# Multi-query attention on one core: quads of heads, values scaled on VectorE, a staged start and a re-planned order

## The chip, the cores and the metric

One core of a Trainium2 chip. The time is device microseconds of one execution; a kernel's time is the median over its runs. Lower is better. All engines named below are those of the one core: PE (TensorE, matrix products), ACT (ScalarE, exponentials), DVE (VectorE), POOL (GpSimd) and SP (SyncE, which here only issues transfers).

## The reference

Eight batches, sequence 1024, 16 query heads of 64 dimensions, and one key head and one value head that all query heads share. In fp32:

```python
scores = np.matmul(q, k.transpose(0, 1, 3, 2)) / np.sqrt(head_dim)     # q: 8x16x1024x64
weights = np.exp(scores - np.max(scores, axis=-1, keepdims=True))
weights = weights / np.sum(weights, axis=-1, keepdims=True)
attn_out = np.matmul(weights, v)
```

The order of the keys within a batch doesn't matter to the result, as long as values stand in the same order.

## The kernel before

The 16 heads of a batch are taken as 8 pairs; over 8 batches that is 64 pairs (`NP`). A pair's keys are cut in 8 tiles of 128, so there are 512 key tiles, numbered through. A tile's scores for a pair (128 keys by 2 heads by 1024 queries) come in two query halves `c` of 512 queries each, 1024 halves in all.

**One half.** `score` (L382) makes two products, one per head, into one of three score slots in PSUM (`sc0` to `sc2`). An exponential then turns the slot into fp16 weights `wt`: on ScalarE by one ACTIVATE (`exp_act`, L397), or on VectorE (`exp_dve`, L402): `z` for each half (L410), and after the second half four more steps for the whole tile (L421 to L428). A tile on VectorE gives three terms (`wt`, `z`, `m`), which are multiplied with three copies of the values that are scaled by the constants `TERMS`.

**Values.** `value` (L431) multiplies weights with values for a group of 6, 4 or 6 of the 16 blocks of 128 queries (`BLOCKS`), and adds up in one of two accumulators in PSUM. Row 65 of the values is a constant, so the sum of the weights comes with it. A ScalarE tile costs one such product per block, a VectorE tile three. When a group is complete, `reciprocal` (L451) and `normalise` (L456) on VectorE write `osb`, and after the third group SP stores the pair. In the last pair each group is stored by itself.

**The order.** PE, ScalarE and VectorE run in an order that is written out by hand: `plan` (L51) walks through the work with its own costs and due times for each instruction (the constants of L22 to L37), decides which tiles VectorE takes (`vtiles`), and emits scores, exponentials, steps, value products and normalisations sorted by due time. `LAG`, `END` and `END_LAG` say how far value work stays behind the scores, `BACKLOG` and `BACK_END` how much work may stand before VectorE, `LAST` how many last tiles VectorE may not take, `MARGIN` and `WAIT` when PE changes between scores and values. The last 8 tiles (`NKT`) are taken by halves: first all first halves, then all second halves (L105 to L112). On the chip each engine runs its list in order and waits where it must.

**Loads.** They are not in the hand-written order; a scheduler places them on SP and POOL. `begin(w)` (L484) runs when the first score of pair `w` is emitted: it loads pair `w+3` (`load_q`, L331, on POOL, with conversion to fp16), transposes pair `w+2` by DMA (`trans_q`, L341, on SP), and in pairs 2, 4 and 5 of a batch brings the next batch's keys (`load_k`, L299, twice into both halves of the rows, so that each head of a pair has its copy), values (`load_v`, L308) and scaled values (`scale_v`, L313, three instructions on POOL). Keys and values are read with key `c*128 + p` on partition `p`, that is in rows of 64 numbers (256 bytes).

**The start.** `load_first` (L349) brings the first keys and the first pair's queries in fp32 by SP and ACT; beside them pairs 1 and 2 and the first values are loaded. `turn_first` (L360) converts both on VectorE (L364, L367), transposes them on PE into the two accumulator banks (L375, L378), and copies them out on VectorE (keys, L376) and ScalarE (queries, L380).

Of the kernel before, what the change touches and what calls it, by code (L numbers as in the profile page):

```python
# [9 lines left out]
FP32 = mybir.dt.float32  # L10
# [13 lines left out]
MARGIN, WAIT = 0.2, 0.2  # L24
END, END_LAG = 5.0, 0.0
# [5 lines left out]
BACKLOG, BACK_END = 5.6, 3.4  # L31
LAST = 14
WBUFS = 25
ZBUFS = 6
LAG = 1.55
# [15 lines left out]
def plan(NP, NKT):  # L51
# [31 lines left out]
    while p < NP or groups:  # L83
        assert min(pe, dve) < 2e3
        if pe <= dve:
# [161 lines left out]
def kernel(  # L247
# [21 lines left out]
    qp = ctx.enter_context(tc.tile_pool(name="qp", bufs=4))  # L269
    qtp = ctx.enter_context(tc.tile_pool(name="qtp", bufs=3))  # L270
# [28 lines left out]
    def load_k(b):  # L299

        st = kst.setdefault(b, {})
        st["k16"] = kvp.tile([P, NKT, 2, D], FP16, tag="k16", name=f"k16{b}")
        for r in range(2):
            nc.gpsimd.dma_start(  # L304
                out=st["k16"][:, :, r, :], in_=k[b].rearrange("(c p) d -> p c d", p=P)
            )

    def load_v(b):  # L308
        st = kst[b]
        st["vn"] = kvp.tile([P, NKT, D], FP32, tag="vn", bufs=1, name=f"vn{b}")  # L310
        nc.sync.dma_start(out=st["vn"], in_=v[b].rearrange("(c p) d -> p c d", p=P))

    def scale_v(b):  # L313
# [3 lines left out]
        for x, c in zip(st["v"], TERMS):  # L317
            if c == 1.0:
                nc.gpsimd.tensor_copy(out=x[:, :, 0:D], in_=st["vn"])  # L319
            else:  # L320
                nc.gpsimd.tensor_scalar(  # L321
                    out=x[:, :, 0:D], in0=st["vn"], scalar1=c, scalar2=None, op0=ALU.mult)
# [7 lines left out]

    def load_q(p):  # L331
        if p >= NP or p in qn:
            return
        b, hp = divmod(p, HP)
        qn[p] = qp.tile([P, NKT, 2 * D], FP16, tag="qn", name=f"qn{p}")
        nc.gpsimd.dma_start(  # L336
            out=qn[p],
            in_=q[b, :, 2 * hp : 2 * hp + 2, :].rearrange("(c p) h d -> p c (h d)", p=P),
        )

    def trans_q(p):  # L341
        if p >= NP:
            return
        qt[p] = qtp.tile([P, NKT + 1, P], FP16, tag="qt", name=f"qt{p}")[:, 0:NKT, :]
        nc.sync.dma_start_transpose(
            out=qt[p], in_=qn[p].rearrange("p c x -> p (c x)")
        )

    def load_first():  # L349
        st = kst.setdefault(0, {})  # L350
        st["kn"] = osbp.tile([P, NKT, D], FP32, tag="osb", name="kn")
        nc.sync.dma_start(out=st["kn"], in_=k[0].rearrange("(c p) d -> p c d", p=P))
        st["qf"] = osbp.tile([P, NKT, 2 * D], FP32, tag="osb", name="qf")
        for c in range(NQC):
# [3 lines left out]
            )  # L358

    def turn_first():  # L360
        st = kst[0]
        k16 = kvp.tile([P, NKT, 2, D], FP16, tag="k16", name="k160")
        for r in range(2):
            nc.vector.tensor_copy(out=k16[:, :, r, :], in_=st["kn"])  # L364
        qn[0] = qp.tile([P, NKT, 2 * D], FP16, tag="qn", name="qn0")
        for c in range(NQC):
            nc.vector.tensor_copy(  # L367
                out=qn[0][:, 4 * c : 4 * c + 4, :], in_=st["qf"][:, 4 * c : 4 * c + 4, :]
            )
# [3 lines left out]
        qt[0] = qtp.tile([P, NKT + 1, P], FP16, tag="qt", name="qt0")[:, 0:NKT, :]  # L373
        for c in range(NKT):
            nc.tensor.transpose(kps[:, c, :], k16[:, c, :, :].rearrange("p r d -> p (r d)"), ident)  # L375
        nc.vector.tensor_copy(out=st["k2t"], in_=kps)  # L376
        for c in range(NKT):
            nc.tensor.transpose(qps[:, c, :], qn[0][:, c, :], ident)  # L378
            if c % 4 == 3:
                nc.scalar.copy(out=qt[0][:, c - 3 : c + 1, :], in_=qps[:, c - 3 : c + 1, :])  # L380
# [103 lines left out]
    def begin(w):  # L484
        load_q(w + 3)
        trans_q(w + 2)
# [63 lines left out]
```

The softmax here doesn't subtract the row's maximum and nothing guards it: scores larger than these inputs give would overflow.

## Time and profile before

| what | value |
|---|---|
| median of 12 runs | 774.1 us (772.11 to 776.3) |
| profiled execution, its own time | 775.15 us |
| its span on the core | 773.4 us |
| PE busy | 734.2 us (95%) |
| DVE busy | 714.4 us (92%) |
| ACT busy | 756.3 us (98%) |
| POOL busy | 108.4 us (14%) |
| exponentials on ScalarE / `z` on VectorE | 820 / 204 |

A line of the timeline gives the start and the length in us, the engine, the line of the code, the operation, output and inputs with shapes, how many instructions are merged, and in brackets how long the engine was idle just before and what released it. A row of the groups gives busy time, the mean ns of one instruction, and the idle time before the group. Instructions of one engine overlap, so a mean duration is longer than the pace at which they follow each other.

### The profile page before, as it was taken

How to read it: one execution, taken by the hardware profiler on the slowest of the kernel's cores; microseconds unless marked ns; L12 is line 12 of the kernel's file. 1: busy time of each engine (PE TensorE's matmuls, PEld its weight loads, DVE VectorE, ACT ScalarE, POOL GpSimd, SP SyncE). 2: the span in 40 equal slices, each digit the busy share in tenths (PEclk: the TensorE clock that was granted, in tenths of full speed). 3: DMA queues.
4: the chain of work that ended last, by engine and by line, in shares of the span. 5: the costliest groups of instructions: out<-in, count | busy, mean ns of one | idle time of the engine just before them, and what ended most of it. 6: DMA issues, size and time to landing. Idle time of an engine off the chain costs nothing.

```text
span 773.4 us, 29898 instructions
## 1 busy us (share of the span) xinstructions
PE 734.2 (95%) x13520; PEld 489.1 (63%) x13520; DVE 714.4 (92%) x1001; ACT 756.3 (98%) x823; POOL 108.4 (14%) x113
## 2 busy tenths in 40 slices
PE   5999999999999999999999999999999999999997
PEld 1466666566666666566666676665666676666675
DVE  5999999999899998998999999999999989999972
ACT  6999999999999999999999999999999999999997
POOL 6500013000130101200013001030001201000000
PEclk9999999999999999999999999999999999999999
DMA  9945586355875457665694545764546465741322
GB/s 153 134 70 98 83 125 115 78 99 97 98 121 106 79 97 121 102 97 71 111 124 84 97 86 83 125 114 67 97 80 115 98 104 78 110 99 43 84 57 83
DMA packets 231137, 75.07 MB, mean 97 GB/s; under 512 B 164449, under 2 KB 231009, under 8 KB 231009
## 3 DMA queue, kind: packets, MB, share of 16 engines
q1 hardware_dynamic: 149600, 54.15, 32.0%
q0 software_dynamic: 80080, 18.36, 26.2%
q8 instruction: 105, 1.72, 0.9%
q10 hardware_dynamic: 1328, 0.66, 0.3%
q14 instruction: 24, 0.19, 0.1%
HBM read 39.58 MB, written 33.55 MB: 95 GB/s over the span
## 4 chain that ended last, share of the span: by engine, by line
ACT 55%; PE 17%; DVE 15%; issue 11%; DMA 1%; ACTq 0%; DVEq 0%
ACT wt L398 55%; PE acc L441 9%; PE sc L386 8%; DVE z L410 6%; DVE m L427 2%; DVE m L428 2%; DVE wt L421 2%; DVE u L424 2%; DVE osb L463 2%; DMA qf<-in_q_dram 1%; DVE rec L454 0%; DVE qn L367 0%; PE qps L378 0%; ACT qt L380 0%; ACTq L355 0%
## 5 line engine op out<-in xcount | busy, mean ns | idle before, releaser
L398 ACT ACTIVATE wt<-sc 128x1024 f16<-128x1024 f32 x820 | 753.9, 1238 | 5.2 <-PE sc L386 4.9
L441 PE MATMUL acc<-vals,wt 128*128 128x65 f16 x8192 | 378.4, 194 | 1.1 <-DVE osb L463 0.8
L441 PEld LDWEIGHTS <-wt 128*128 128x128 f16 x8192 | 296.1, 97 | 125.5 <-issue 124.9
L386 PE MATMUL sc<-qt,k2t 64*128 64x512 f16 x2048 | 349.1, 388 | 27.0 <-ACT wt L398 15.6
L410 DVE TENSOR_SCALAR z<-sc 128x1024 uint16<-128x1024 f32 x204 | 249.0, 1220 | 22.5 <-PE sc L386 20.0
L386 PEld LDWEIGHTS <-k2t 64*128 64x128 f16 x2048 | 107.6, 94 | 107.0 <-issue 61.2
L336 POOL DMA_DIRECT2D qn<-in_q_dram x63 | 58.7, 932 | 550.0 <-DMA qt<-qn 517.7
L427 DVE TENSOR_TENSOR m<-u 128x2048 f16<-128x2048 f16 x102 | 124.6, 1222 | 1.8
L428 DVE TENSOR_TENSOR m<-z,m 128x2048 f16<-128x2048 f16 x102 | 123.1, 1207 | 0.4
L441 PE MATMUL acc<-vals,z 128*128 128x65 f16 x1632 | 100.1, 194 | 0.0
L463 DVE TENSOR_TENSOR osb<-acc,rec 128x384 f32<-128x384 f32 (+1 forms) x192 | 97.2, 506 | 1.3
L441 PE MATMUL acc<-vals,m 128*128 128x65 f16 x1632 | 98.2, 193 | 0.0
L441 PEld LDWEIGHTS <-z 128*128 128x128 f16 x1632 | 69.2, 97 | 19.5 <-issue 19.5
L441 PEld LDWEIGHTS <-m 128*128 128x128 f16 x1632 | 68.3, 97 | 20.7 <-issue 20.7
L424 DVE TENSOR_SCALAR u<-z 128x2048 uint16<-128x2048 uint16 x102 | 73.6, 721 | 0.0
L421 DVE TENSOR_SCALAR wt<-z 128x2048 uint16<-128x2048 uint16 x102 | 71.1, 697 | 2.1 <-ACT wt L398 0.4
L454 DVE RECIPROCAL rec<-acc 128x6 f32<-128x6 f32 (+1 forms) x192 | 35.1, 183 | 21.4 <-PE acc L441 21.3
L321 POOL TENSOR_SCALAR vals<-vn 128x512 f16<-128x512 f32 x16 | 28.3, 1771 | 26.3 <-PE acc L441 23.7
L304 POOL DMA_DIRECT2D k<-in_k_dram x14 | 13.3, 956 | 0.2 <-issue 0.2
L319 POOL CAST vals<-vn 128x512 f16<-128x512 f32 x8 | 7.5, 939 | 3.6 <-DMA vn<-in_v_dram 3.5
L375 PE MATMUL kps<-ident,k 128*128 128x128 f16 x8 | 1.0, 311 | 6.0 <-DVE k L364 6.0
L380 ACT COPY qt<-qps 128x512 f16<-128x512 f16 x2 | 1.2, 586 | 5.0 <-PE qps L378 5.0
(14 smaller groups left out, 8.0 us busy)
## 6 DMA issues: line engine op xcount, KB each, us to landing
out_dram<-osb SPq DMA_DIRECT2D x63, 512.0 KB, 3.5
qn<-in_q_dram POOLq DMA_DIRECT2D x63, 256.0 KB, 4.7
vn<-in_v_dram SPq DMA_DIRECT2D x8, 256.0 KB, 3.2
k<-in_k_dram POOLq DMA_DIRECT2D x14, 128.0 KB, 6.0
qt<-qn SPq DMA_TRANSPOSE x63, 3.8
qf<-in_q_dram ACTq DMA_DIRECT2D x2, 256.0 KB, 5.4
out_dram<-osb SPq DMA_DIRECT2D x2, 192.0 KB, 2.1
kn<-in_k_dram SPq DMA_DIRECT2D x1, 256.0 KB, 4.4
```

The costliest lines, as they stand in the source:

```text
L321: nc.gpsimd.tensor_scalar(out=x[:, :, 0:D], in0=st["vn"], scalar1=c, scalar2=None, op0=ALU.mult)
L336: nc.gpsimd.dma_start(out=qn[p], in_=q[b, :, 2 * hp : 2 * hp + 2, :].rearrange("(c p) h d -> p c (h d)", p=P),)
L386: nc.tensor.matmul(sc[t, c][:, h, :], kst[p // HP]["k2t"][64 * h : 64 * h + 64, j, :], qt[p].rearrange("p c x -> p (c x)")[64 * h : 64 * h ...
L398: nc.scalar.activation(out=wt[t][:, :, c * QC : (c + 1) * QC], in_=sc.pop((t, c)), func=EXP, scale=ascale)
L410: nc.vector.tensor_scalar(out=z[:, :, c * QC : (c + 1) * QC], in0=sc.pop((t, c)), scalar1=vscale, scalar2=(15 + math.log2(C0)) * ONE, op0= ...
L421: lambda: V.tensor_scalar(out=wt[t].bitcast(U16), in0=z, scalar1=0xFC00, scalar2=None, op0=ALU.bitwise_and),
L424: lambda: V.tensor_scalar(out=u, in0=z, scalar1=1023, scalar2=14 << 10, op0=ALU.bitwise_and, op1=ALU.bitwise_or),
L427: lambda: V.tensor_tensor(out=m, in0=h, in1=h, op=ALU.mult),
L428: lambda: V.tensor_tensor(out=m, in0=z.bitcast(FP16), in1=m, op=ALU.mult),
L441: nc.tensor.matmul(acc[p, grp][:, o : o + D + 1], w[:, h, i * P : (i + 1) * P], kst[p // HP]["v"][k][:, j, 0 : D + 1], start=(n == 0 and o ...
L454: nc.vector.reciprocal(out=rec[p, grp][:, 0 : a.shape[1]], in_=a[:, :, D])
L463: nc.vector.tensor_tensor(out=o.rearrange("p i (h d) -> p (i h) d", h=2)[:, BLOCKS[grp] : BLOCKS[grp + 1], :], in0=a[:, :, 0:D], in1=rec.p ...
```

## The change

- **Constants of the planner**: `MARGIN`, `WAIT`, `END`, `END_LAG`, `BACKLOG`, `BACK_END`, `LAG` get other values, and a new `SPLIT` of 4 takes the place of 8 for the number of last tiles that are taken by halves.
- **Quads**: pairs 0 and 1 are still moved singly; from pair 2 on, one load and one DMA transpose bring two pairs (4 heads), at every second pair. The loads run `w+4`, the transposes `w+2` ahead. Buffers: two of double size, for loaded and for transposed queries each (4 and 3 single ones before). The score reads its queries as four pieces of 128.
- **Rows of keys and values**: key `p*8 + c` on partition `p`, so that a partition's 8 keys are one row of 2 KB. The same in values.
- **Scaling of values**: three instructions on VectorE in the hand-written order in place of three on POOL; the first batch's at the start of pair 1.
- **Start**: POOL converts one half of the first keys, VectorE the other. Keys and queries are transposed and copied by halves, keys' copies on ScalarE, queries' on VectorE. The loads of pair 1 and of the first values wait for the first keys and the first query half, because POOL copies one element of these into their buffers; the load of pairs 2 and 3 comes after the transposes.
- **POOL** is now in the hand-written order too.

```diff
-MARGIN, WAIT = 0.2, 0.2
-END, END_LAG = 5.0, 0.0
+MARGIN, WAIT = 0.29, 0.18
+END, END_LAG = 4.84, 0.175
...
-BACKLOG, BACK_END = 5.6, 3.4
-LAST = 14
+BACKLOG, BACK_END = 5.67, 4.09
+LAST, SPLIT = 14, 4
...
-LAG = 1.55
+LAG = 1.37
...
-                if nt < NT - NKT:
+                if nt < NT - SPLIT:
...
-    qp = ctx.enter_context(tc.tile_pool(name="qp", bufs=4))
-    qtp = ctx.enter_context(tc.tile_pool(name="qtp", bufs=3))
+    qp = ctx.enter_context(tc.tile_pool(name="qp", bufs=2))
+    qtp = ctx.enter_context(tc.tile_pool(name="qtp", bufs=2))
...
-                out=st["k16"][:, :, r, :], in_=k[b].rearrange("(c p) d -> p c d", p=P)
+                out=st["k16"][:, :, r, :], in_=k[b].rearrange("(p c) d -> p c d", p=P)
...
         for x, c in zip(st["v"], TERMS):
-            if c == 1.0:
-                nc.gpsimd.tensor_copy(out=x[:, :, 0:D], in_=st["vn"])
-            else:
-                nc.gpsimd.tensor_scalar(
-                    out=x[:, :, 0:D], in0=st["vn"], scalar1=c, scalar2=None, op0=ALU.mult)
+            nc.vector.tensor_scalar(
+                out=x[:, :, 0:D], in0=st["vn"], scalar1=c, scalar2=None, op0=ALU.mult)
...
+    def quad(p):
+
+        return (p,) if p < 2 else (p & ~1, p | 1)
+
+    def queries(pool, tag, p, more):
+
+        t = pool.tile([P, 2 * NKT + more, P], FP16, tag=tag, name=f"{tag}{p}")
+        return t[:, 0 : NKT * len(quad(p)), :]
...
     def trans_q(p):
...
+        ps = quad(p)
+        t = queries(qtp, "qt", p, 1)
         nc.sync.dma_start_transpose(
-            out=qt[p], in_=qn[p].rearrange("p c x -> p (c x)")
-        )
+            out=t, in_=qn[ps[0]].rearrange("p c x -> p (c x)")
+        )
+        for r, x in enumerate(ps):
+            qt[x] = t.rearrange("p (c r) x -> p c r x", r=len(ps))[:, :, r, :]
...
+        nc.gpsimd.tensor_copy(out=st["k16"][:, :, 1, :], in_=kn)
...
+        for x, y in ((qn[1][:, 0, 0:1], kn), (st["vn"][:, 0, 0:1], st["qf"])):
+            nc.gpsimd.tensor_copy(out=x, in_=y[:, 0, 0:1])
...
+        nc.vector.tensor_copy(out=k16[:, :, 0, :], in_=st["kn"])
+        for c in range(NQC):
+            x = slice(4 * c, 4 * c + 4)
+            for i in range(4 * c, 4 * c + 4):
+                nc.tensor.transpose(
+                    kps[:, i, :], k16[:, i, :, :].rearrange("p r d -> p (r d)"), ident)
+            nc.scalar.copy(out=st["k2t"][:, x, :], in_=kps[:, x, :])
+            nc.vector.tensor_copy(out=qn[0][:, x, :], in_=st["qf"][:, x, :])
+            for i in range(4 * c, 4 * c + 4):
+                nc.tensor.transpose(qps[:, i, :], qn[0][:, i, :], ident)
+            nc.vector.tensor_copy(out=qt[0][:, x, :], in_=qps[:, x, :])
...
-                qt[p].rearrange("p c x -> p (c x)")[
-                    64 * h : 64 * h + 64, c * QC : (c + 1) * QC
-                ],
+                qt[p][64 * h : 64 * h + 64, 4 * c : 4 * c + 4, :],
...
     def begin(w):
-        load_q(w + 3)
-        trans_q(w + 2)
+        if w % 2 == 0:
+            if w + 4 < NP:
+                load_q(w + 4)
+            if w + 2 < NP:
+                trans_q(w + 2)
+        if w == 1:
+            scale_v(0)
...
     load_first()
+    load_v(0)
     load_q(1)
-    load_v(0)
-    load_q(2)
-    trans_q(1)
-    scale_v(0)
-    with tc.manual_schedule(engines={ENG.PE, ENG.Activation, ENG.DVE}):
+    with tc.manual_schedule(engines={ENG.PE, ENG.Activation, ENG.DVE, ENG.Pool}):
         turn_first()
+        load_q(2)
+        trans_q(1)
```

More of the change, by code (lines that the diff above doesn't have):

```diff
@@ L309, in load_v @@
         st = kst[b]
-        st["vn"] = kvp.tile([P, NKT, D], FP32, tag="vn", bufs=1, name=f"vn{b}")
-        nc.sync.dma_start(out=st["vn"], in_=v[b].rearrange("(c p) d -> p c d", p=P))
+        if "vn" not in st:
+            st["vn"] = kvp.tile([P, NKT, D], FP32, tag="vn", bufs=1, name=f"vn{b}")
+        nc.sync.dma_start(out=st["vn"], in_=v[b].rearrange("(p c) d -> p c d", p=P))
     def scale_v(b):
@@ L329, in trans_k @@
         )
+    def quad(p):
[3 more added lines that the diff above has]
+        return t[:, 0 : NKT * len(quad(p)), :]
     def load_q(p):
[L332 to L335, printed above, removed]
+        ps = quad(p)
+        b, hp = divmod(ps[0], HP)
+        if p not in qn:
+            qn[p] = queries(qp, "qn", p, 0)
         nc.gpsimd.dma_start(
[L337 to L338 removed]
+            out=qn[ps[0]].rearrange("p (c r) x -> p c (r x)", r=len(ps)),
+            in_=q[b, :, 2 * hp : 2 * hp + 2 * len(ps), :].rearrange(
+                "(c p) h d -> p c (h d)", p=P),
         )
     def trans_q(p):
[L342 to L344 removed]
+        ps = quad(p)
+        t = queries(qtp, "qt", p, 1)
         nc.sync.dma_start_transpose(
[L346 removed]
+            out=t, in_=qn[ps[0]].rearrange("p c x -> p (c x)")
         )
+        for r, x in enumerate(ps):
+            qt[x] = t.rearrange("p (c r) x -> p c r x", r=len(ps))[:, :, r, :]
     def load_first():
         st = kst.setdefault(0, {})
[L351 to L352 removed]
+        kn = osbp.tile([P, NKT, D], FP32, tag="osb", name="kn")
+        nc.sync.dma_start(out=kn, in_=k[0].rearrange("(p c) d -> p c d", p=P))
         st["qf"] = osbp.tile([P, NKT, 2 * D], FP32, tag="osb", name="qf")
@@ L358, in load_first @@
             )
+        st["k16"] = kvp.tile([P, NKT, 2, D], FP16, tag="k16", name="k160")
+        nc.gpsimd.tensor_copy(out=st["k16"][:, :, 1, :], in_=kn)
+        st["kn"] = kn
+        qn[0] = queries(qp, "qn", 0, 0)
+        qn[1] = queries(qp, "qn", 1, 0)
+        st["vn"] = kvp.tile([P, NKT, D], FP32, tag="vn", bufs=1, name="vn0")
+        for x, y in ((qn[1][:, 0, 0:1], kn), (st["vn"][:, 0, 0:1], st["qf"])):
+            nc.gpsimd.tensor_copy(out=x, in_=y[:, 0, 0:1])
+        qt[0] = queries(qtp, "qt", 0, 1)
     def turn_first():
         st = kst[0]
[L362 to L368, printed above, removed]
-            )
+        k16 = st["k16"]
         kps = psp.tile([P, NKT, P], FP16, tag="acc0", name="kps")
@@ L372, in turn_first @@
         st["k2t"] = kvp.tile([P, NKT + 1, P], FP16, tag="k2t", name="k2t0")[:, 0:NKT, :]
[L373 to L380, printed above, removed]
+        nc.vector.tensor_copy(out=k16[:, :, 0, :], in_=st["kn"])
[9 more added lines that the diff above has]
+            nc.vector.tensor_copy(out=qt[0][:, x, :], in_=qps[:, x, :])
     def score(t, c, s):
```

## The prediction

> **What bounds the kernel now.** I read the page from its first part (busy shares), then the ScalarE rows of the timeline, then the idle-time column of the groups, then the start and the end of the timeline.
>
> ```profile
> span 773.4 us, 29898 instructions
> PE 734.2 (95%) x13520; PEld 489.1 (63%) x13520; DVE 714.4 (92%) x1001; ACT 756.3 (98%) x823; POOL 108.4 (14%) x113
> ...
> L398 ACT ACTIVATE wt<-sc 128x1024 f16<-128x1024 f32 x820 | 753.9, 1238 | 5.2 <-PE sc L386 4.9
> ...
> L410 DVE TENSOR_SCALAR z<-sc 128x1024 uint16<-128x1024 f32 x204 | 249.0, 1220 | 22.5 <-PE sc L386 20.0
> ...
> L454 DVE RECIPROCAL rec<-acc 128x6 f32<-128x6 f32 (+1 forms) x192 | 35.1, 183 | 21.4 <-PE acc L441 21.3
> ```
>
> ScalarE (ACT) is busy 98% and waits 5.2 us in all; the two large waits of VectorE (DVE) cost nothing as long as ScalarE is fed. The 1238 ns of one exponential is not its pace, since instructions overlap. The pace comes from the unbroken runs of the ScalarE timeline:
>
> ```profile
> 31.54 130.44 ACT L398 ACTIVATE wt<-sc 128x1024 f16<-128x1024 f32 x142 [0.32 <-PE sc L386]
> 162.15 108.27 ACT L398 ACTIVATE wt<-sc 128x1024 f16<-128x1024 f32 x118 [0.17 <-PE sc L386]
> 271.19 152.79 ACT L398 ACTIVATE wt<-sc 128x1024 f16<-128x1024 f32 x166 [0.77 <-PE sc L386]
> 424.40 3.77 ACT L398 ACTIVATE wt<-sc 128x1024 f16<-128x1024 f32 x4 [0.42 <-PE sc L386]
> 428.32 16.66 ACT L398 ACTIVATE wt<-sc 128x1024 f16<-128x1024 f32 x18
> 446.38 90.86 ACT L398 ACTIVATE wt<-sc 128x1024 f16<-128x1024 f32 x99 [1.40 <-PE sc L386]
> 552.00 216.44 ACT L398 ACTIVATE wt<-sc 128x1024 f16<-128x1024 f32 x236 [0.17 <-PE sc L386]
> ```
>
> The last run has 236 exponentials in 216.44 us; the shortest one takes 1.02, so the other 235 cost (216.44 - 1.02)/235 = 0.9166 us each. The exponentials fill 9.39 (first start) to 768.44 (552.00 + 216.44), 759.05 us. At full pace 820 need 1.02 + 819 x 0.9166 = 751.7, so 7.3 us are stalls. The span is thus start 9.39, exponentials 751.7, stalls 7.3, tail 773.4 - 768.44 = 5.0. I forecast each of the four.
>
> **Exponentials: -5.5 us.** The planner's new constants fix another written order. In the built order VectorE takes 105 of 512 tiles where it took 102, so ScalarE has 814 exponentials: 6 x 0.9166 = 5.5 less.
>
> **Stalls of the old order: -3.5 us.** Counting exponentials along the runs, those after the 164th, 282nd, 448th, 470th and 584th pause. At these places the planner's own due times for ScalarE leave gaps: its order brings the score late there. The new due times have no gap. What they cost is taken from the trace: recorded waits 0.17 + 0.77 + 0.42 + 1.40 + 0.17 = 2.93, and an exponential after a pause doesn't overlap its forerunner, which hides about 0.1 more each: 3.5. The other 3.8 us of stalls (2.0 of them before 34 us, the rest around a clock dip at 540 us and short waits) I leave as they are.
>
> **VectorE: heavier, the price is in the bursts.** It gets
> - 3 more tiles. The five rows of an exponential by VectorE sum to 249.0 + 124.6 + 123.1 + 73.6 + 71.1 = 641.4 us for 102 tiles, 6.29 each; overlap cuts that (all rows sum to 776, busy is 714.4, factor 0.92) to 5.8: +17.4 us.
> - 24 value scalings that GpSimd (POOL) did. No row of VectorE has them; the nearest is the two conversions of the same shape (128x512 f32 to f16) at the start, 0.76 for two, so 0.38 each: +9.1 us, in eight bursts of three, 1.1 us each. Bounds 0.34 and 0.53 each.
> - Relief: written orders that put an instruction right behind the one whose result it needs cost 0.11 (m by m at 407.06 comes 1.25 after the one at 405.81 whose result it reads; with an unrelated neighbour 1.14). Of such pairs the built order has 123 before and 19 after: 104 x 0.11 = -11.4.
> - Relief from GpSimd. In the trace u takes 1.09 beside a value scaling at 409.21 on GpSimd and 0.65 without:
>
> ```profile
> 403.52 0.65 DVE L424 TENSOR_SCALAR u<-z 128x2048 uint16<-128x2048 uint16 x1
> ...
> 409.21 1.61 POOL L321 TENSOR_SCALAR vals<-vn 128x512 f16<-128x512 f32 x1 [7.90 <-PE acc L441]
> ...
> 410.28 1.09 DVE L424 TENSOR_SCALAR u<-z 128x2048 uint16<-128x2048 uint16 x1
> ```
>
> By the row, the excess of mean over median is (721 - 684) x 102 = 3.8 us for u and (697 - 686) x 102 = 1.1 for wt: -4.9. The Trainium skill, "SBUF — State Buffer", section "Who interferes with whom", states that a VectorE instruction in a two-port mode and a GpSimd instruction exclude each other for the whole instruction. Taken at its most, all 28.3 + 7.5 = 35.8 us of GpSimd's scaling block VectorE, and the move would make it lighter by 35.8 - 9.1 = 26.7; by the row it becomes heavier by 9.1 - 4.9 = 4.2. I take the row: most of those 35.8 us lie beside instructions that the trace shows undisturbed.
>
> Sum for VectorE: 17.4 + 9.1 - 11.4 - 4.9 = +10.2 us. Between 32 and 745 us it is busy 681.2 of 713, so 31.8 idle; that window shrinks by 9 (5.5 + 3.5), and the remaining idle is about 12.6 us, under 2%. So VectorE keeps up on average, but has nothing to spare behind a burst. What is queued behind one is the next z on VectorE, which holds one of three score slots in PSUM; PE's next score for that slot waits, and PE is in order, so the scores for ScalarE behind it are late. Bounds: 0 (idle time of VectorE takes every burst) and 8 x 1.1 = 9 (each reaches ScalarE whole). ScalarE has up to two finished scores ahead of it, so I take a quarter, nearer the lower end: +2. If that cover is gone it is 9.
>
> **Start: -1.7 us.** Now the chain is qf, cast, transposes, copy, score:
>
> ```profile
> 5.17 0.76 DVE L364 CAST k<-kn 128x512 f16<-128x512 f32 x2 [5.17 <-DMA kn<-in_k_dram]
> ...
> 7.37 0.72 DVE L367 CAST qn<-qf 128x512 f16<-128x512 f32 x1 [1.10 <-DMA qf<-in_q_dram]
> ...
> 8.79 0.59 ACT L380 COPY qt<-qps 128x512 f16<-128x512 f16 x1 [0.72 <-PE qps L378]
> ...
> 9.39 9.27 ACT L398 ACTIVATE wt<-sc 128x1024 f16<-128x1024 f32 x10
> ```
>
> Keys land at 5.15 and the second query half at 7.34, in company with values and two more query loads. In the changed order those wait (one-element copies on GpSimd that read kn and qf), and the keys come in 2 KB rows instead of 256 B. A value load of the same bytes in 256 B rows lands in 3.0 at best (issue to landing of vn: 3.0/3.2/5.9), so keys at 0.73 + 3.0 = 3.7 and query halves at 4.3 and 4.9. The Trainium skill, "DMA: Bandwidth & Descriptors", section "Anatomy of one DMA", gives 2.0 us plus bytes over 436 GB/s: an estimate of 2.6 for 256 KB, keys at 3.3, exponentials 0.4 earlier than by the row. I take the row. From there: GpSimd cast 0.60 (4.3), four key transposes 0.6 (4.9), ScalarE copies half 0.59 (5.5), PE's next key transposes wait for that copy (their line waits on ACT) and end at 6.1; VectorE meanwhile does k, first query cast, first qt copy and second query cast, about 6.4; the last query transposes 0.6 (7.05), and the scores stand behind them in PE's queue; from there to the first exponential 0.65 as now (8.74 to 9.39): 7.7. Bounds: 6.9 (DMA estimate, no queueing) and 9.4 (no gain).
>
> What is late next: the pair-1 queries issue only when qf is there, at about 5 (now 1.42), plus about 1 to issue, 4.7 to land, 1.3 + 3.8 to be transposed, 15.8; pair 1 starts 10.8 us after the first scores, at about 18. Hidden, with 2 us to spare. The first values land by 10, the first value matmul is at 22 or later. The quads (two pairs per load and transpose) halve GpSimd's and SP's issues. In SP's queue a double transpose stands behind stores; it is released when pair w-1 is scored and needed two pairs (23 us) later, against 2 x 3.8 us: hidden, price 0. The score's moving operand is now four pieces of 128; PE waits 27 us before scores anyway, 0.
>
> **Tail: +1.5 us.** Splitting only four last tiles leaves more value work behind the last score: in the built order 128 matmuls (all of pair 63's) instead of 68.
>
> ```profile
> 765.61 0.60 PE L386 MATMUL sc<-qt,k2t 64*128 64x512 f16 x4
> ...
> 766.15 2.09 PE L441 MATMUL acc<-vals,wt 128*128 128x65 f16 x60
> ...
> 768.49 0.42 PE L441 MATMUL acc<-vals,wt 128*128 128x65 f16 x8 [0.26 <-ACT wt L398]
> ```
>
> PE ends 3.3 after the last score now; 60 matmuls take 2.09, so 128 take 4.5, plus 0.53 of scores: 5.0. ScalarE ends about 2.5 after that score, against 2.8. PE thus ends 2.5 after ScalarE instead of 0.5: +2.0. Behind it only one group is normalised instead of two: -0.5. The store of 3.3 us remains.
>
> **Sum.** -5.5 - 3.5 + 2 - 1.7 + 1.5 = -7.2: span 766.2. The profiled run took 775.15 us for 773.4; the runs' median 774.1 is 0.7 over the span, which I keep: 766.9.
>
> **Rivals.**
> 1. Everything is covered: bursts 0 and the start at its lower bound (6.9, -0.8): 764.1. For it: 21.4 us of VectorE's idle is waiting for acc, which is time left over. Against it: those waits stand in the middle of its queue and need not meet a burst.
> 2. The start doesn't get shorter (keys' arrival isn't what ends last, GpSimd's cast and the single file on PE are): first exponential at 9.4 and bursts at half: 766.9 + 1.7 + 2.5 = 771.1. For it: PE's order puts all sixteen transposes ahead of the first score, and one copy between.
> 3. Slower: VectorE becomes the bound. Place: every z behind a burst, in all batches. If the two reliefs don't come (16.3 us), its need rises by 26.5 against 31.8 - 9 = 22.8 of idle, 3.7 too much; and if half of the old idle cannot be filled, since it is waiting for acc or scores, 16 more: stalls +19.7 in place of +2, so 784.6 at worst, 776.6 with 8 of the 16. It decides from 2 + 7.2 = 9.2 us of new stalls on. Against it: the 1.09 beside GpSimd and the 0.11 of dependence are in the trace.
>
> **How the numbers follow.** Chances: the sum above 0.55 (its own range 764.8 to 769), rival 1 0.16, rival 2 0.14, rival 3 0.15. The range runs from 762.5 (a little under rival 1, whose bounds don't add up lower than that by more than 2) to 772.5 (above rival 2), and leaves rival 3 out. 0.2% is 1.5 us, about what tells two times of this kernel apart; within it 0.03, taken from rival 2's upper end and rival 3's lower one: faster 0.84, same 0.03, slower 0.13.
>
> **What would show it.** First exponential at 7.7 and the landing of kn and qf; 814 exponentials at 0.917, no pause after the 164th, 282nd or 470th; three scalings of 0.38 on VectorE and, just behind, ScalarE pauses of a few tenths; u never above 0.8 beside GpSimd except near its DMA issues; PE ending 2.5 after the last exponential. The forecast is wrong if ScalarE shows waits for scores all along the run (then z is late), or if pair 1 or 2 waits for its qt.

## The result and the profile after

The changed kernel takes 765.39 us (median of 8 runs, 764.61 to 767.2) against 774.66 of the kernel before, run beside it: ratio 0.9881, 95% interval 0.9865 to 0.9896. It is 1.2% faster. The forecast was 766.9, with a range of 762.5 to 772.5.

The page of the changed kernel, the lines that answer to those of before (engines, then groups as busy time, mean ns, idle time before them):

```profile
span 764.1 us, 29940 instructions
PE 739.0 (97%) x13616; PEld 486.6 (64%) x13616; DVE 721.3 (94%) x1043; ACT 750.3 (98%) x817; POOL 47.0 (6%) x61
...
L411 ACT ACTIVATE wt<-sc 128x1024 f16<-128x1024 f32 x814 | 747.8, 1244 | 2.3 <-PE sc L401 2.0
...
L423 DVE TENSOR_SCALAR z<-sc 128x1024 uint16<-128x1024 f32 x210 | 256.4, 1221 | 19.2 <-PE sc L401 14.5
...
L467 DVE RECIPROCAL rec<-acc 128x6 f32<-128x6 f32 (+1 forms) x192 | 35.1, 183 | 13.7 <-PE acc L454 13.7
...
L319 DVE TENSOR_SCALAR vals<-vn 128x512 f16<-128x512 f32 x24 | 8.7, 419 | 0.0
```

ScalarE is still busy 98%, with 6 exponentials fewer; VectorE has become busier (94% after 92%). ScalarE's own timeline, all exponentials:

```profile
8.14 13.86 ACT L411 ACTIVATE wt<-sc 128x1024 f16<-128x1024 f32 x15 [0.67 <-PE sc L401]
22.30 1.02 ACT L411 ACTIVATE wt<-sc 128x1024 f16<-128x1024 f32 x1 [0.31 <-PE sc L401]
23.71 2.92 ACT L411 ACTIVATE wt<-sc 128x1024 f16<-128x1024 f32 x3 [0.39 <-PE sc L401]
26.91 87.55 ACT L411 ACTIVATE wt<-sc 128x1024 f16<-128x1024 f32 x95 [0.27 <-PE sc L401]
114.62 139.79 ACT L411 ACTIVATE wt<-sc 128x1024 f16<-128x1024 f32 x152 [0.16 <-PE sc L401]
254.65 502.95 ACT L411 ACTIVATE wt<-sc 128x1024 f16<-128x1024 f32 x548 [0.24 <-PE sc L401]
```

The breaks of 0.8 and 1.4 us that stood at 271 and 446 us are gone. The exponentials fill 8.14 to 757.60 (254.65 + 502.95), 749.46 us. At the pace of before 814 of them need 1.02 + 813 x 0.9166 = 746.2, which leaves 3.25 of stalls. At the start the keys are there at 4.02, where they came at 5.17; at the end PE has 128 products left behind the last score, and ends (759.98) 2.4 after the last exponential:

```profile
4.02 0.43 DVE L385 CAST k<-kn 128x512 f16<-128x512 f32 x1 [4.02 <-DMA kn<-in_k_dram]
...
755.83 4.15 PE L454 MATMUL acc<-vals,wt 128*128 128x65 f16 x128
```

The four terms of the prediction, in us of the profiled executions:

| term | before | after | difference | forecast |
|---|---|---|---|---|
| start (first exponential) | 9.39 | 8.14 | -1.25 | -1.7 |
| exponentials at full pace | 751.7 | 746.2 | -5.5 | -5.5 |
| stalls of ScalarE | 7.3 | 3.25 | -4.1 | -1.5 (-3.5 and +2) |
| tail after the last exponential | 5.0 | 6.5 | +1.5 | +1.5 |
| span | 773.4 | 764.1 | -9.3 | -7.2 |

The forecast was 2.1 us short: 2.6 too little in the stalls, less 0.45 too much at the start. The experiments ask which part of the change made each term.

"Full pace" needs care: 0.9166 is the mean of a long run without a large break, not ScalarE's own step. Taken singly from the trace, the starts mostly follow each other at 0.904 us (536 of 819 steps before and 424 of 813 after are below 0.907). Longer steps go with late scores: they average 0.93 us or more where the score's products ended less than 0.12 us before the exponential's start, and 0.905 to 0.912 where they ended over 0.2 before. At 0.904 the exponentials take 741.4 and 736.0 us and the stalls are 17.7 and 13.5. The differences in the table hold (-5.4 and -4.2), but some 10 us of mostly such small waits are inside its pace.

### The profile page after: what moved, and what is told of

Read it like the earlier page. It is cut to its first block, busy times and chain, and to the rows that moved or that the text cites. A ratio compares the mean times of both kernels' runs of the same rounds, so it can differ in the third digit from the quotient of the medians.

```text
span 764.1 us, 29940 instructions
## 1 busy us (share of the span) xinstructions
PE 739.0 (97%) x13616; PEld 486.6 (64%) x13616; DVE 721.3 (94%) x1043; ACT 750.3 (98%) x817; POOL 47.0 (6%) x61
## 4 chain that ended last, share of the span: by engine, by line
ACT 43%; PE 35%; DVE 16%; issue 5%; DMA 0%; POOL 0%; DVEq 0%; ACTq 0%
ACT wt L411 43%; PE acc L454 20%; PE sc L401 14%; DVE z L423 6%; DVE m L441 2%; DVE m L440 2%; DVE osb L476 2%; DVE u L437 1%; DVE wt L434 1%; DVE vals L319 1%; DVE rec L467 0%; DMA kn<-in_k_dram 0%; PE qps L394 0%; POOL k L369 0%; PE kps L389 0%
## 5 line engine op out<-in xcount | busy, mean ns | idle before, releaser
L401 PE MATMUL sc<-qt,k2t 64*128 64x512 f16 x2048 | 356.6, 388 | 13.9 <-ACT wt L411 6.5
L423 DVE TENSOR_SCALAR z<-sc 128x1024 uint16<-128x1024 f32 x210 | 256.4, 1221 | 19.2 <-PE sc L401 14.5
L401 PEld LDWEIGHTS <-k2t 64*128 64x128 f16 x2048 | 100.8, 93 | 99.6 <-issue 55.1
L441 DVE TENSOR_TENSOR m<-z,m 128x2048 f16<-128x2048 f16 x105 | 126.5, 1205 | 0.0
L454 PE MATMUL acc<-vals,z 128*128 128x65 f16 x1680 | 103.2, 194 | 0.0
L454 PE MATMUL acc<-vals,m 128*128 128x65 f16 x1680 | 94.4, 194 | 0.0
L437 DVE TENSOR_SCALAR u<-z 128x2048 uint16<-128x2048 uint16 x105 | 71.1, 677 | 0.0
L343 POOL DMA_DIRECT2D qn<-in_q_dram x32 | 30.6, 956 | 614.4 <-DMA qt<-qn 613.0
L319 DVE TENSOR_SCALAR vals<-vn 128x512 f16<-128x512 f32 x24 | 8.7, 419 | 0.0
```

The source lines that it names most:

```text
L319: nc.vector.tensor_scalar(out=x[:, :, 0:D], in0=st["vn"], scalar1=c, scalar2=None, op0=ALU.mult)
L343: nc.gpsimd.dma_start(out=qn[ps[0]].rearrange("p (c r) x -> p c (r x)", r=len(ps)), in_=q[b, :, 2 * hp : 2 * hp + 2 * len(ps), :].rearrang ...
L401: nc.tensor.matmul(sc[t, c][:, h, :], kst[p // HP]["k2t"][64 * h : 64 * h + 64, j, :], qt[p][64 * h : 64 * h + 64, 4 * c : 4 * c + 4, :], ...
L423: nc.vector.tensor_scalar(out=z[:, :, c * QC : (c + 1) * QC], in0=sc.pop((t, c)), scalar1=vscale, scalar2=(15 + math.log2(C0)) * ONE, op0= ...
L437: lambda: V.tensor_scalar(out=u, in0=z, scalar1=1023, scalar2=14 << 10, op0=ALU.bitwise_and, op1=ALU.bitwise_or),
L441: lambda: V.tensor_tensor(out=m, in0=z.bitcast(FP16), in1=m, op=ALU.mult),
```

## Experiments

Three sets of four kernels; each set ran on one chip beside the kernel before. The changed kernel itself came out at 0.9881 and, in the second set, at 0.9905, so ratios are compared within a set, and differences of 0.1% to 0.2% are read from the terms of the profile rather than from the ratio. Only the second set held the changed kernel itself; in the first and the third, its nearest kin (without the waits, and with single pairs) stand for it.

### The order alone

The kernel before with nothing but the planner's new constants and `SPLIT`:

```diff
-MARGIN, WAIT = 0.2, 0.2
-END, END_LAG = 5.0, 0.0
+MARGIN, WAIT = 0.29, 0.18
+END, END_LAG = 4.84, 0.175
...
-BACKLOG, BACK_END = 5.6, 3.4
-LAST = 14
+BACKLOG, BACK_END = 5.67, 4.09
+LAST, SPLIT = 14, 4
...
-LAG = 1.55
+LAG = 1.37
...
-                if nt < NT - NKT:
+                if nt < NT - SPLIT:
```

> Only the planner's constants and SPLIT of the change, on the old loads, old start and GpSimd scaling. My theory (the four terms add up): 814 exponentials -5.5 us, the pauses of the old order -3.5, tail +1.5, start unchanged at 9.4: span about 766, ratio to before 0.990. Rival (the denser order only works if GpSimd's scaling no longer disturbs VectorE): new pauses of ScalarE behind every scaling on GpSimd, span 770 or more, ratio 0.995 or more.

Measured: 765.56 us, ratio 0.9881 (0.9868 to 0.9895), span 763.2. ScalarE's timeline in it:

```profile
9.13 9.27 ACT L398 ACTIVATE wt<-sc 128x1024 f16<-128x1024 f32 x10
18.63 4.70 ACT L398 ACTIVATE wt<-sc 128x1024 f16<-128x1024 f32 x5 [0.23 <-PE sc L386]
23.48 1.02 ACT L398 ACTIVATE wt<-sc 128x1024 f16<-128x1024 f32 x1 [0.16 <-PE sc L386]
24.90 731.79 ACT L398 ACTIVATE wt<-sc 128x1024 f16<-128x1024 f32 x798 [0.39 <-PE sc L386]
```

From 24.90 on, 798 exponentials run without a break: (731.79 - 1.02)/797 = 0.9169 each. Stalls are 756.69 - 9.13 - 746.2 = 1.35 us, all before 30 us, though GpSimd still scales the values. (The start is 0.26 earlier than in the profile of before, with the same instructions: that much the landing of the first loads scatters.) The rival falls: the new order needs no relief from GpSimd. It alone is worth the whole gain of the change: in the same set the changed kernel without its waits has 0.9884, and everything but the order, below, 1.0003. More of the stalls go than the 3.5 that I had credited it with: 7.3 - 1.35 = 6.0.

`plan` is plain Python, and run by itself it tells more. The old constants leave seven gaps between ScalarE's due times, 4.8 us in all: 0.49 after the 164th exponential, 1.01 after the 282nd, 0.21 (344th), 0.57 (448th), 1.86 (470th), 0.15 (482nd) and 0.49 (584th). The new constants leave none. Put back one at a time, `END_LAG` and `BACKLOG` don't alter the order, and `END`, `BACK_END` and `SPLIT` alter only its end; `MARGIN`, `WAIT` and `LAG` each bring gaps back, and with these three alone new there is no gap. No run separates them on the chip.

### Everything but the order

The changed kernel with the old constants and the old split put back (the diff above, reversed, on the new loads, start and scaling).

> The whole change except its order: old constants, last eight tiles split. My theory: start -1.25 us as measured, the pauses of the old order come back, VectorE's scaling bursts find more idle time than in the new order and cost 0 to 1: span 772 to 773, ratio 0.998 to 0.999. Rival (the gain is in the loads and in the scaling): span 769 or less, ratio 0.994.

Measured: 774.6 us, ratio 1.0003 (0.9994 to 1.0012), span 772.8.

```profile
27.80 132.80 ACT L411 ACTIVATE wt<-sc 128x1024 f16<-128x1024 f32 x144 [0.29 <-PE sc L401]
160.78 2.86 ACT L411 ACTIVATE wt<-sc 128x1024 f16<-128x1024 f32 x3 [0.17 <-PE sc L401]
164.26 105.94 ACT L411 ACTIVATE wt<-sc 128x1024 f16<-128x1024 f32 x115 [0.63 <-PE sc L401]
270.97 152.58 ACT L411 ACTIVATE wt<-sc 128x1024 f16<-128x1024 f32 x166 [0.77 <-PE sc L401]
423.78 20.27 ACT L411 ACTIVATE wt<-sc 128x1024 f16<-128x1024 f32 x22 [0.23 <-PE sc L401]
446.10 96.39 ACT L411 ACTIVATE wt<-sc 128x1024 f16<-128x1024 f32 x105 [2.05 <-PE sc L401]
542.79 8.47 ACT L411 ACTIVATE wt<-sc 128x1024 f16<-128x1024 f32 x9 [0.29 <-PE sc L401]
551.43 216.44 ACT L411 ACTIVATE wt<-sc 128x1024 f16<-128x1024 f32 x236 [0.17 <-PE sc L401]
```

The first lines of this timeline, not shown, hold 15 + 4 + 1 = 20 exponentials. Counted on, breaks stand after the 164th, 282nd, 448th, 470th and 584th, the very places of the kernel before, with other loads, other buffers and another start. They belong to the order. Two more, after the 167th and the 575th, follow scalings on VectorE (from 158.1 and 536.8 us). The first exponential is at 8.01, but stalls are 8.15: the earlier start (-1.4) is given back partly in stalls (+0.8), and no difference in time is left to see. The span lies in my 772 to 773; the ratio reached neither the rival's 0.994 nor my 0.998. Loads, start and scaling together are worth nothing that can be seen.

### Scaling on GpSimd again

```diff
-            nc.vector.tensor_scalar(
-                out=x[:, :, 0:D], in0=st["vn"], scalar1=c, scalar2=None, op0=ALU.mult)
+            if c == 1.0:
+                nc.gpsimd.tensor_copy(out=x[:, :, 0:D], in_=st["vn"])
+            else:
+                nc.gpsimd.tensor_scalar(
+                    out=x[:, :, 0:D], in0=st["vn"], scalar1=c, scalar2=None, op0=ALU.mult)
```

> The changed kernel with the scaling of values back on GpSimd. My theory (VectorE gets 4 us lighter in sum, the bursts of 1.1 us fall away but each scaling slows one or two VectorE instructions by 0.4): ScalarE's stalls of 3.3 us change by -1.5 to +1, ratio to before 0.987 to 0.990. Rival (exclusion of the two engines for whole instructions): VectorE is blocked for most of GpSimd's 36 us, with 18 us of idle left in the middle of the run: stalls +5 us or more, ratio 0.994 or more.

Measured: 764.04 us, ratio 0.9862 (0.9848 to 0.9875), the lowest of its set and a little under what I expected. Stalls are 2.0 in place of 3.25. Its groups:

```profile
L437 DVE TENSOR_SCALAR wt<-z 128x2048 uint16<-128x2048 uint16 x105 | 75.8, 722 | 0.2
...
L322 POOL TENSOR_SCALAR vals<-vn 128x512 f16<-128x512 f32 x16 | 29.6, 1850 | 1.4
```

`wt` takes 722 ns on average, against 684 in the changed kernel: 105 x 0.038 = 4 us of disturbance by GpSimd, about what the row of before gave, and far from the 36 us of GpSimd's work. Between 32 and 735 us VectorE is idle 703 - 683.8 = 19.2 us, against 17.7 with the scaling on VectorE. That VectorE pays for the whole length of GpSimd's work is refuted; whether one of the two stands still while the other works is not decided by these rows. Moving the scaling to VectorE was no gain. By the profile it was a small loss, 1.25 us of stalls, and the breaks behind the bursts are gone; but two profiles of the changed kernel differ by 1.4, and the ratio overlaps that of the kernel without the waits (0.9884) in the same set.

### The start: without the waits

The changed kernel without the two one-element copies:

```diff
-        for x, y in ((qn[1][:, 0, 0:1], kn), (st["vn"][:, 0, 0:1], st["qf"])):
-            nc.gpsimd.tensor_copy(out=x, in_=y[:, 0, 0:1])
```

> The changed kernel without the two one-element copies, so that the loads of pair 1 and of the first values start at once beside the first keys and queries. Theory that the quiet start is what made it earlier: kn and qf land 0.5 to 1.5 us later, first exponential at 8.6 to 9.4 instead of 8.14, ratio 0.989 to 0.990. Rival (the halves and PE's order set the start, not the landing): first exponential within 0.2 of 8.14, ratio 0.988.

Measured: 766.11 us, ratio 0.9884 (0.9869 to 0.9899). The timeline at its start:

```profile
1.21 0.41 SPq L312 DMA_DIRECT2D vn<-in_v_dram  x1
1.43 1.01 POOL L343 DMA_DIRECT2D qn<-in_q_dram  x1 [0.23 <-issue]
...
3.99 0.43 DVE L383 CAST k<-kn 128x512 f16<-128x512 f32 x1 [3.99 <-DMA kn<-in_k_dram]
...
6.41 0.43 DVE L390 CAST qn<-qf 128x512 f16<-128x512 f32 x1
6.85 0.59 ACT L389 COPY k2t<-kps 128x512 f16<-128x512 f16 x1 [0.67 <-PE kps L387]
```

The loads of values and pair 1 start at 1.2 and 1.4 again, and the keys are there at 3.99, as with the waits (4.02). The first exponential is at 8.08. The second query cast starts at 6.41 with no wait for a transfer. The rival holds: the waits do nothing that can be seen for the start.

### The start: short rows

The changed kernel with `"(c p) d -> p c d"` in place of `"(p c) d -> p c d"` in the three reads of keys and values.

> The changed kernel with keys and values read in 256 B rows again (key c*128+p on partition p), all else as changed. Theory that the rows of 2 KB are what brings the keys earlier: kn lands at 4.6 to 5.2 instead of 4.0 and the first exponential moves from 8.1 to 8.6-9.1, ratio to before 0.989 to 0.990. Rival (the halves and the quiet start do it): kn at 4.0 to 4.2, first exponential within 0.2 of 8.1, ratio unchanged against the changed kernel.

Measured: 767.09 us, ratio 0.9918 (0.9903 to 0.9933).

```profile
5.13 0.43 DVE L385 CAST k<-kn 128x512 f16<-128x512 f32 x1 [5.13 <-DMA kn<-in_k_dram]
5.16 0.87 POOL L369 CAST k<-kn 128x512 f16<-128x512 f32 x1 [3.65 <-DMA kn<-in_k_dram]
```

The keys land 4.4 us after their issue (3.3 with rows of 2 KB), and the first exponential moves with them, by 1.0 to 9.16, where the order alone, with the old start, has 9.13. The rows of 2 KB are what the earlier start comes from: 1.0 of the 1.25; the rest is no more than the 0.26 by which the old start scattered. Long rows with the old start, which waited for the second query half, were not run, so what the halves are worth beside long rows stays open.

### The start: the second half of the keys on ScalarE

Scaling on GpSimd as above, and

```diff
-        nc.gpsimd.tensor_copy(out=st["k16"][:, :, 1, :], in_=kn)
...
         nc.vector.tensor_copy(out=k16[:, :, 0, :], in_=st["kn"])
+        nc.scalar.copy(out=k16[:, :, 1, :], in_=st["kn"])
```

> The changed kernel with the scaling on GpSimd and with the second half of the first keys converted on ScalarE (0.59 in the trace for a copy of the shape) instead of on GpSimd (0.87). Theory that GpSimd's conversion is on the path of the start: first exponential at 7.6 to 7.8 instead of 8.1 and, with the bursts gone, stalls about 1.5: span 762, ratio 0.985. Rival (the query half is what ends last): first exponential unchanged, ratio 0.986 as with the scaling on GpSimd alone.

Measured: 765.63 us, ratio 0.9885 (0.9867 to 0.9902), first exponential at 7.87. With the scaling on GpSimd alone it was 7.81, so nothing is gained: the first key transposes do start 0.3 us sooner after the landing (4.53 with keys at 3.86, against 4.97 with keys at 4.02), but the second query cast still waits its turn on VectorE, behind a copy that waits for PE. Inconclusive as a whole: its stalls were 3.3, with single breaks of 0.70, 0.51 and 0.29 at 27, 324 and 534 us; with the scaling on GpSimd alone there are none of that size at these places, but one of 0.75 at 114.

### The tail: eight tiles split

```diff
-LAST, SPLIT = 14, 4
+LAST, SPLIT = 14, 8
```

> The changed kernel with the last eight tiles split by query halves, as before. As the prediction put it (splitting four leaves more value work behind the last score): tail back to 5.0 from 6.5, span -1.5 us. Rival (the rest of the new order leaves that work, the built order still has 128 value matmuls behind the last score): tail 6.5, ratio 0.988.

Measured: 765.75 us, ratio 0.989 (0.9875 to 0.9905), beside 0.9905 (0.989 to 0.9919) of the changed kernel in the same set; tail 764.1 - 757.58 = 6.5, by the last line of its exponentials:

```profile
114.53 643.05 ACT L411 ACTIVATE wt<-sc 128x1024 f16<-128x1024 f32 x700 [0.15 <-PE sc L401]
```

`SPLIT` does nothing. The larger tail comes with the rest of the new order: `plan` leaves 128 value products behind the last score with `SPLIT` at 8 too, 68 with all old constants, and 182 with `MARGIN`, `WAIT` and `LAG` alone new.

> The changed kernel itself, beside the three others on the same chip. 765.4 us, ratio to before 0.988; first exponential at 8.1, stalls 3.3, of them about 1.4 between 22 and 29 us and the rest in steps of some 95 us.

The changed kernel in this set: 766.89 us, first exponential 8.08, stalls 4.6. The 1.4 above its first profile are single breaks: by the brackets 0.5 more at 27 us, 0.6 more at 116, 0.4 new at 674, less 0.24 at 255; the breaks behind the bursts repeat to a tenth, but for that one.

### The bursts on VectorE: spread, doubled, moved

Spread over three pairs:

```diff
-    def scale_v(b):
+    def scale_v(b, terms=(0, 1, 2)):
...
-        for x, c in zip(st["v"], TERMS):
+        for n in terms:
+            x, c = st["v"][n], TERMS[n]
...
-                scale_v(b + 1)
+            if hp >= HP - 3:
+                scale_v(b + 1, (hp - HP + 3,))
```

> The changed kernel with the three scalings of a batch's values on VectorE at three successive pairs instead of in one burst (the first batch's stay together). My theory (a burst of 1.1 us makes the next scores late, one scaling of 0.35 fits into the slack): the pauses in steps of 95 us go, those before 29 us stay, stalls 3.3 to 1.5-2.2, span -1.3 us, ratio 0.9865. Rival (VectorE has too little idle time in sum, whatever the grouping): stalls unchanged at 3.3, ratio 0.988.

Measured: 764.97 us, ratio 0.9878 (0.9861 to 0.9895), 1.9 us less than the changed kernel beside it, the intervals just overlapping. Its stalls are 3.0, not the 1.5 to 2.2 that I expected: 1.9 of them before 30 us, where the changed kernel had 1.4. What a burst does is seen in the changed kernel's timeline of VectorE and ScalarE:

```profile
251.18 0.41 DVE L476 TENSOR_TENSOR osb<-acc,rec 128x256 f32<-128x256 f32 x1
251.51 1.09 DVE L319 TENSOR_SCALAR vals<-vn 128x512 f16<-128x512 f32 x3
252.51 1.22 DVE L440 TENSOR_TENSOR m<-u 128x2048 f16<-128x2048 f16 x1
253.65 0.69 DVE L434 TENSOR_SCALAR wt<-z 128x2048 uint16<-128x2048 uint16 x1
254.37 1.23 DVE L423 TENSOR_SCALAR z<-sc 128x1024 uint16<-128x1024 f32 x1
254.65 1.94 ACT L411 ACTIVATE wt<-sc 128x1024 f16<-128x1024 f32 x2 [0.24 <-PE sc L401]
```

The burst puts off the next `z` by a microsecond, and ScalarE's next exponential waits for its score. From 27.34 us the spread version reads

```profile
27.34 157.15 ACT L412 ACTIVATE wt<-sc 128x1024 f16<-128x1024 f32 x171 [0.39 <-PE sc L402]
185.17 572.10 ACT L412 ACTIVATE wt<-sc 128x1024 f16<-128x1024 f32 x624 [0.69 <-PE sc L402]
```

The breaks in steps of some 95 us are gone. Thirty exponentials behind each of the seven later bursts the changed kernel has lost 0.34, 0.32, 0.35, 0.12, 0.32, 0.13 and 0.12 us against 0.9166 each, 1.7 in all; the order alone, without bursts on VectorE, loses 0.1 in all at these times. A single break at 185 has come. For these breaks the rival, that only the sum counts, falls: the sum of the scalings is the same.

Every scaling done twice:

```diff
+            for _ in range(2):
-            nc.vector.tensor_scalar(
-                out=x[:, :, 0:D], in0=st["vn"], scalar1=c, scalar2=None, op0=ALU.mult)
+                nc.vector.tensor_scalar(
+                    out=x[:, :, 0:D], in0=st["vn"], scalar1=c, scalar2=None, op0=ALU.mult)
```

> The changed kernel with every scaling of values done twice, so that a burst on VectorE takes 2.1 us. My theory (VectorE has about 2% idle and a burst goes through to the scores): each of the eight bursts costs ScalarE 0.5 to 1 us more, stalls from 3.3-4.6 to 8-12, span +4 to +8, ratio 0.994 to 0.999. Rival (VectorE's idle time takes it): under +1.5 us, ratio 0.990.

Measured: 781.64 us, ratio 1.0106 (1.0086 to 1.0125): slower than the kernel before. ScalarE around three of the bursts:

```profile
262.45 1.02 ACT L412 ACTIVATE wt<-sc 128x1024 f16<-128x1024 f32 x1 [1.19 <-PE sc L402]
264.46 90.98 ACT L412 ACTIVATE wt<-sc 128x1024 f16<-128x1024 f32 x99 [0.99 <-PE sc L402]
356.48 1.02 ACT L412 ACTIVATE wt<-sc 128x1024 f16<-128x1024 f32 x1 [1.04 <-PE sc L402]
...
361.52 88.31 ACT L412 ACTIVATE wt<-sc 128x1024 f16<-128x1024 f32 x96 [0.64 <-PE sc L402]
451.78 1.02 ACT L412 ACTIVATE wt<-sc 128x1024 f16<-128x1024 f32 x1 [1.95 <-PE sc L402]
```

Stalls are 20.9 us, where I expected 8 to 12. One more microsecond in a burst costs (20.9 - 3.25)/8 = 2.2 us, while the first one costs 1.7/7 = 0.24 at the seven later bursts. VectorE was idle 18 us of the middle of the run and should have held 8 us more; it had no use of that, since the idle time doesn't lie behind the bursts. PE's lines around one of the bursts show two costs (the last one is a row of a table of stretches: from and to, us, PE's busy us and instructions, and the granted clock, 0.50):

```profile
255.22 0.72 PE L455 MATMUL acc<-vals,wt 128*128 128x65 f16 x18
...
261.92 0.85 PE L402 MATMUL sc<-qt,k2t 64*128 64x512 f16 x4 [1.71 <-DVE z L424]
262.71 1.17 PE L455 MATMUL acc<-vals,wt 128*128 128x65 f16 x18
...
263.00:264.00 1.00, 1.00 (x18) 0.50 0.00 0
```

PE's next score waits 1.71 us for the late `z`. And when PE goes on, its clock is down: the trace has it at half for 3.4 us behind six of the eight bursts (from 71.0, 262.2, 357.7, 449.9, 548.9 and 644.4 us), and the same 18 value products take 1.17 us in place of 0.72. In the changed kernel the clock stays at full from 26 us to the end of PE's work. Thirty exponentials behind these six bursts 2.5 to 2.9 us are lost, behind the one in the middle of the run that the clock survived (162 us) 1.7. By this one comparison, about 1 us of what a doubled burst costs comes with the lower clock, an estimate, and the rest with the late `z`.

Spread, and the first batch's three moved from the start of pair 1 to just behind the first `z`:

```diff
-        if w == 1:
-            scale_v(0)
...
             elif op == "z":
+                if tuple(args) == (0, 1):
+                    scale_v(0)
                 exp_dve(*args)
```

> A version meant to be better than both: scalings of later batches spread over three pairs as in the run before, and the first batch's three put behind the first z, where VectorE waits 1.1 us for the next score anyway. Theory that the burst at 18.8 us costs the start of the run: the pauses before 30 us shrink from 1.4-1.9 to about 1, stalls about 2, span 763, ratio 0.986. Rival (these pauses come from PE's first change to value products, not from the burst): pauses before 30 us unchanged, ratio 0.9875.

Measured: 763.48 us, ratio 0.9874 (0.9858 to 0.9891), span 761.5, the lowest time of all runs and the lowest of its set (the others 766.4 and more).

```profile
8.01 14.77 ACT L412 ACTIVATE wt<-sc 128x1024 f16<-128x1024 f32 x16 [0.59 <-PE sc L402]
22.94 2.92 ACT L412 ACTIVATE wt<-sc 128x1024 f16<-128x1024 f32 x3 [0.16 <-PE sc L402]
26.11 728.91 ACT L412 ACTIVATE wt<-sc 128x1024 f16<-128x1024 f32 x795 [0.24 <-PE sc L402]
```

Stalls are 0.8 us, less than I expected; the ratio is that of the rival, in a set where the kernel before ran at 773.35. No break is left behind a burst, and between 30 and 745 us ScalarE loses nothing against 0.9166, as in the order alone. Before 30 us it loses 0.7 in place of 1.4. The moved burst need not be the only cause of that. In every run the value products up to some 25 to 30 us are slow, as these two lines of the changed kernel show:

```profile
22.62 0.51 PE L454 MATMUL acc<-vals,wt 128*128 128x65 f16 x6
...
26.80 0.35 PE L454 MATMUL acc<-vals,wt 128*128 128x65 f16 x6
```

One starts 54 ns after the other in the first line, and 29 in the second; the trace's first full clock is recorded between them, at 26.0. It is at 25.1 here, at 24.5 with the scaling on GpSimd (stalls before 30 us 0.7 too), at 27.6 with single pairs (2.6) and at 30.3 in the kernel before (2.0). The early stalls go roughly with the time at which PE's clock comes up, and no run separates it from the burst. By the profile this version is 2.6 us better than the changed kernel. Their ratios overlap, and no set held both, so the size of that gain is not settled; the missing breaks behind the bursts are.

### Single pairs in place of quads

```diff
-        return (p,) if p < 2 else (p & ~1, p | 1)
+        return (p,)
...
-        if w % 2 == 0:
-            if w + 4 < NP:
-                load_q(w + 4)
-            if w + 2 < NP:
-                trans_q(w + 2)
+        if w + 3 < NP:
+            load_q(w + 3)
+        if w + 2 < NP:
+            trans_q(w + 2)
```

(and single buffers, 4 for loaded and 3 for transposed queries)

> The changed kernel with every pair loaded and transposed by itself again (three pairs ahead for loads, two for transposes, 4 and 3 single buffers). My theory (hidden transfers, price 0): same time within 0.7 us, ratio 0.988 to 0.990. Rival (half as many issues on GpSimd disturb VectorE less, that is part of the gain): stalls of ScalarE +1.5 us or more, ratio 0.991 or more.

Measured: 766.37 us, ratio 0.9909 (0.9894 to 0.9924), beside 0.9918 of the short rows in the same set; stalls 4.2, of them 2.6 before 30 us and 1.2 in the middle, where the breaks are those of the bursts, and one of 0.5 at 288 us. The quads are hidden, price and worth 0, as far as 0.2% can tell.

## Why the prediction was right, point by point

- **What bounds it** (ScalarE at 0.9166 us per exponential): right in the engine and in the mean, which 798 exponentials at 0.9169 repeat in the order alone. But it is no full pace: ScalarE's own step is 0.904, and the order alone has it in only 335 of 813 steps. That its mean agrees to a thousandth is in part chance.
- **Exponentials, -5.5**: right. The six exponentials were counted in the built order; at the same pace the rest is arithmetic.
- **"Stalls of the old order: -3.5"**: mechanism right, size too small. The order alone takes away 6.0. I credited five breaks; the due times have seven, 4.8 us in all, and that is near the 5.0 us of stalls in the middle of the run before, which fall to 0 with the new order. For the five I took the idle times in the brackets, 2.93, and 0.1 each for the lost overlap. From start to start they lose 4.2 (0.54, 1.07, 0.53, 1.66 and 0.39 over the pace), so the lost overlap is 0.25 each. The rest I put down to the clock dip at 540 us and short waits and left; it went as well. The trace of the order alone has no dip. Whether the order keeps the clock up, or the profiled execution was merely spared, is open.
- **"VectorE: heavier, the price is in the bursts", +2**: right in kind and nearly in size for the single bursts. Against the order alone, the changed kernel has 3.25 - 1.35 = 1.9 more stalls, nearly all of it between 30 and 745 us: the bursts, and a break at 114 us that stands behind none. Wrong was the price beyond the cover, "9 if that cover is gone": doubling the bursts cost 17.7, since PE waits for the late `z` and then runs at a lower clock, which the prediction had at nothing. VectorE's busy time rose by 721.3 - 714.4 = 6.9, forecast 10.2. The line given for the 0.11 of dependence doesn't show it: a reciprocal stands between the two `m` (at 406.94) and takes those 0.1. The size is right all the same: in the trace of before, `u` is followed by its own `m` after 0.72 us and by another instruction after 0.60. The row was the right choice over the bound drawn from the Trainium skill, "SBUF — State Buffer", section "Who interferes with whom": there the engine that issues second waits for the other's whole instruction, which need not be VectorE, and GpSimd's scaling costs VectorE's `wt` 4 us, not 36.
- **"Start: -1.7"**: size near (-1.25), cause wrong. The step "those wait ... and the keys come in 2 KB rows" named two causes; the rows are 1.0 of the 1.25, and the waits nothing. The keys landed in 3.3 us, after 3.0 by the row. The estimate of 2.6 from the Trainium skill, "DMA: Bandwidth & Descriptors", section "Anatomy of one DMA", was further off; that section fits its figures to transfers that GpSimd issues, and SP issued this one. What is missing of the 1.7 is these 0.3 and GpSimd's cast, 0.87 and not 0.60.
- **"Tail: +1.5"**: size right, cause wrong. 128 matmuls took 4.15 us and PE ended 2.4 after the last exponential (2.5 forecast). But splitting four tiles is not what leaves them behind: with eight split the tail is the same. The 128 were counted in the whole new order, so the size had to come out.
- **"Quads ... hidden, price 0"**: right, as far as 0.2% can tell.
- **Rivals**: none came. Rival 3's place is real: at twice the burst the kernel is slower than before, though not because VectorE has too much work in sum: between 32 and 745 us it is idle 713 - 689.2 = 23.8 us there.

The total came as near as it did by some luck: the stalls of the old order were 2.5 too small, the start 0.45 too large and for half the wrong reason.

## What to carry to other kernels

When the engine that sets the time runs back to back, split its window in count times pace, stalls, start and tail, and look at single steps too, since a mean pace hides small waits. Try the written order alone before the moved work: here the constants of the order are the whole gain, and three rebuilt parts beside them add up to nothing. Where an order is planned, its own due times tell where it will pause. Work that is put on an almost full engine in one piece can be cheap at one size (1.1 us here) and dear at twice that size, when other engines wait for it; give it in small pieces or where that engine waits anyway. Two changes made at one place (quiet start and long rows) need a run each before one of them is given the credit.

## What the runs showed of the hardware that was not expected

- The same 256 KB of keys land 3.3 us after the issue with rows of 2 KB and 4.4 with rows of 256 B. Other transfers beside them (values and pair 1's queries) made no difference: 3.2.
- In two pairs of overlapping conversions of 128x512 the one that began later was the longer. Before, GpSimd's from 7.20 on took 0.60, and VectorE's from 7.37 on 0.72; after, VectorE's from 4.02 on took 0.43, and GpSimd's from 4.05 on 0.87.
- PE's clock fell to half for 3.4 us behind six of the eight doubled bursts, after waits of PE of 1.4 to 1.8 us.
- Single breaks of 0.4 to 0.9 us of ScalarE stand at places that differ from run to run of the same kernel (674 us in one, none there in another). They make up to 1.4 us of a profiled span. The one at 25 to 28 us is missing in two of the three runs where the clock was full by 25.2 us, and loses 0.8 to 0.9 in those where it came up at 26.6 or later (the doubled bursts aside); what makes the others stays open.
